# A two-layer decoder trunk on one core: unread 16-column products ahead of fifteen groups of products, and the norm's matrix moved by 64 bytes

## The chip, the cores and the metric

The kernel runs on one core of one Trainium2 chip. The time is that of one execution on the device, in microseconds (us); of several executions the median is taken. Most executions of this kernel agree within 0.3%.

## The reference, cut to what matters

One sequence of 512 tokens of width 1024 goes through two layers, all in float32.

```
h = rmsnorm(x, g) * (1 + scale) + shift            # scale, shift, gate: from c, one matrix-vector product per layer
layer 0: q, k, v, g = split(h @ w_in)              # 4 heads, q and k 256 wide, v and g 512 wide
         y = retention(rope(q), rope(k), v)        # chunked recurrence, here as scores over the whole sequence
         x = x + gate * ((silu(g) * groupnorm(y)) @ w_out)
layer 1: q, k = silu(causal_conv(h @ w_qk)); v, o  # stabilised mLSTM, 4 heads of the same widths
         x = x + gate * (groupnorm(sigmoid(o) * y) @ w_out)
both:    a, b = split(causal_conv(rmsnorm(x) ... @ w_up)); x = x + gate * ((silu(a) * b) @ w_down)
return rmsnorm(x, final_g)
```

## The kernel before, in words

Every float32 operand of a large product is split in two parts, high and low, of a rounded kind that TensorE takes in one pass (`hi`, `lo`; tiles `whi` and `wlo` for weights, `hh` and `hl` for the normed input, `t24h`, `t3h` and their low parts for sums of it). A product of 128x128 by 128x256 or by 128x512 is three instructions: high by high, high by low, low by high. In a profile row `out<-moving,stationary` the second name is the matrix that is loaded into the array before the product (LDWEIGHTS, rows of PEld), and the first is the operand that streams through it.

Most projections are done by a scheme with seven half-size products in place of eight (`seven`, `FoldUse`, `PairStream`, `ValueStream`; order of the products 1, 2, 6, 5, 7, 4, 3). A pair of 128-column tiles of query, key or gate weights is one such scheme with the weights stationary (output tiles `p1` and `p2`, shown as `p`). The values of a head are two such schemes side by side with the input stationary and the weights moving (output tiles `pv`). Each is 7 x 12 = 84 instructions of 256 columns. A head's queries and keys are two schemes after each other, 168 instructions; so are its gates, and so are its values. `heads` strings the heads together: queries, values, scores (`psc`), gates, attention (`pav`), output products (`po`). In the feed-forward part the same scheme runs for 18 tile pairs in `folded`. `boundary` does the last output products of a part in two halves of 256 columns and computes the next norm beside them: `SquareSum.root` multiplies the sums of squares by a constant matrix with 1/1024 in every cell (`ones["d"]`, tile `ones_d`, output `pms`), two instructions for each half.

In memory the input tiles (`slots`) and the constants start at multiples of 256 bytes. The weight tiles of the schemes, of `boundary` and of the products after it (`pf`) lie 64 bytes behind such a multiple: the tiles have 64 spare columns (`WPAD`) and are used from column 16 on (`OFF`). `ones_d` starts at a multiple of 256 bytes.

Two places already hold a product of 16 columns whose result nobody reads (`short_product`): the first scheme of each `folded` writes one into the quarter of its second output bank that VectorE fills later, and each `boundary` writes one into the last 16 columns of its first output bank.

The order of all instructions is made before the program is built, by a planner in the file (`Plan`): it plays the program through with a cost for each instruction, gives every instruction that feeds TensorE a due time, and lets each engine take what is due. Eight PSUM banks are handed out in turn; an instruction that reads a bank is due before the first product into the bank eight turns later.

Of the kernel before, what the change touches and what calls it, by code (L numbers as in the profile page):

```python
# [11 lines left out]
F32R = mybir.dt.float32r  # L12
# [4 lines left out]
P = 128  # L17
# [18 lines left out]
WPAD = 64  # L36
OFF = 16
# [349 lines left out]
def trunk(ctx: ExitStack, tc: tile.TileContext, xT, cb, pos, vec, ident, decay, zmask, ada, w_s0, w_in0, w_v0,  # L387
          w_o0, w_in1, w_v1, w_f1, w_o1, w_up, w_dn, out):
    nc = tc.nc
    const = ctx.enter_context(tc.tile_pool(name="const", bufs=1))  # L390
# [14 lines left out]
    def tile_of(pool, shape, dt, tag, name):  # L405
        return Buf(pool, shape, dt, tag, name, KINDS.get(tag, 0), tag == "ps")

    def slot(s, dt=F32, w=T):
        return tile_of(slots, [P, w], dt, "s", uid(s))
# [10 lines left out]
    def fixed(pool, shape, dt, name):  # L420
        b = tile_of(pool, shape, dt, name, name)
        b.get()
        return b

    plan = Plan()
    V, A, G, PE, S = (plan.engine(*p) for p in (("DVE", nc.vector), ("ACT", nc.scalar), ("POOL", nc.gpsimd),
                                                ("PE", nc.tensor), ("SP", nc.sync)))
# [3 lines left out]
    V.memset(fixed(const, [P, 32], F32, "pad")[:], 0.0)  # L431
    ones = {}
    for name, v in (("d", 1.0 / D), ("v", 1.0 / DV), ("1", 1.0)):
        o = fixed(const, [P, P], F32R, f"ones_{name}")
        V.memset(o[:].bitcast(F32), v)
        ones[name] = o

# [221 lines left out]
    def short_product(o, w, b):  # L659


        PE.matmul(o, w, b, start=True, stop=True, skip_group_check=True)

    def mm2(o, w, b, r=slice(None), start=True, stop=True):
        PE.matmul(o, w, b.hi[:, r], start=start, stop=False)
# [110 lines left out]
    class PairStream:  # L776
# [5 lines left out]
        def open(self, folds):  # L782
            self.f = folds
            b1, b2 = self.banks = bank("p1"), bank("p2")
            self.c11, self.c12, self.c21, self.c22 = b1[:, HA], b1[:, HB], b2[:, HA], b2[:, HB]

        def product(self, n, o, start):
            hi, hc, lo, lc = self.f.p[n]
            for k in range(4):
                b = self.terms(n, k)  # L790
                st, sp = start and k == 0, n in (2, 3, 4) and k == 3
                ch, cl = hi[:, hc + k * P : hc + k * P + P], lo[:, lc + k * P : lc + k * P + P]
                PE.matmul(o, ch, b[0], start=st, stop=False, skip_group_check=True)
                PE.matmul(o, ch, b[1], start=False, stop=False, skip_group_check=True)
                PE.matmul(o, cl, b[0], start=False, stop=sp, skip_group_check=True)

    class ValueStream(PairStream):
# [7 lines left out]
        def open(self, f):  # L805
            self.f = f
            x_, y_ = self.banks = bank("pv"), bank("pv")
            self.c11, self.c21, self.c12, self.c22 = x_[:, HA], x_[:, HB], y_[:, HA], y_[:, HB]

        def product(self, n, o, start):  # L810
            ts = slice(self.t * P, self.t * P + P)
            hi, lo = self.f.p[n]
            for k in range(4):
                b = self.terms(n, k)
                st, sp = start and k == 0, n in (2, 3, 4) and k == 3
                cs = slice(k * 256, k * 256 + 256)
                PE.matmul(o, b[0][:, ts], hi[:, cs], start=st, stop=False, skip_group_check=True)
                PE.matmul(o, b[0][:, ts], lo[:, cs], start=False, stop=False, skip_group_check=True)
                PE.matmul(o, b[1][:, ts], hi[:, cs], start=False, stop=sp, skip_group_check=True)

    def seven(use, streams, done, between=lambda j: None):


        fs = []

        def mk(n):
            def fn(w):
                if n == ORDER[0]:
                    for s in streams:
                        s.open(w[0])  # L830
                        fs.append(slot("fs"))
                for s, f in zip(streams, fs):
                    o = {1: s.c21, 2: s.c11, 5: s.c12, 3: s.c12}.get(n, s.c21)
                    s.product(n, o, n in s.starts)
                    if n in (1, 6, 7):
                        A.copy(f[:, HB if n == 6 else HA], s.c21)
                    if n == 7:
                        V.tensor_tensor(s.c22, s.c12, f[:, HA], op=ALU.add)
                    elif n == 2:
                        V.tensor_tensor(s.c11, s.c11, f[:, HA], op=ALU.add)  # L840
                    elif n == 3:
                        V.tensor_tensor(s.c12, s.c12, f[:, HB], op=ALU.add)
                if n == 3:
                    done(*[s.banks for s in streams])
            return fn
        for j, n in enumerate(ORDER):
            item([use], mk(n), j in FREE_STEPS)
            between(j)

    def fold_pairs(srcs, terms, thens, between=lambda j: None):  # L850

        def each(then):
            def done(bs):
                for b in bs:
                    then(b)
            return done
        for n, (src, then) in enumerate(zip(srcs, thens)):
            seven(FoldUse(src, n), [PairStream(terms, then)], each(then), lambda j: between(7 * n + j))

    def fold_values(src, terms, v, split, between=lambda j: None):  # L860

        def done(a, b):
            for ps in (a[0], b[0], a[1], b[1]):
                split(v, ps)
        seven(ValueFoldUse(src, 0), [ValueStream(terms, t) for t in range(2)], done, between)

    def folded(folds, h, terms, pairs, downs, quota):

# [668 lines left out]
    def ret_gate(i):  # L1537
        def then(ps):
            g = slot("g")
            A.activation(g[:], ps[:], AF.Silu)  # L1540
            R[i]["g"].append(g)
        return then
# [162 lines left out]
    sums0 = Sums(h0, {}, 0, 0)  # L1705

    def sums_early():
        sums0.make()
        sums0.turn()

    def pair_srcs(w, at):
        return [(w[at], w[at + 1]), (w[at + 2], w[at + 3])]

    def ret_q(i, between=nothing):
        thens = [half_pair(R[i], name, rope) for name in ("q", "k")]
        if i:
            fold_pairs(pair_srcs(w_in0, i * 8), sums0.terms, thens, between)
            return
        for n, then in enumerate(thens):
            for j in range(2):  # L1720
                proj_item(w_in0[i * 8 + 2 * n + j], h0, then, 2 * n + j in QLOW)
        item([], lambda w: sums_early())

    def ret_g(i):
        fold_pairs(pair_srcs(w_in0, i * 8 + 4), sums0.terms, [ret_gate(i)] * 2)

    def ret_v(i, between=nothing):
        fold_values(w_v0[i - 1], sums0.terms, R[i]["v"], center_split, between)
# [90 lines left out]
    def ml_gate(i):  # L1819
        def then(ps):  # L1820
            o = slot("o")
            A.activation(o[:], ps[:], AF.Sigmoid)
            M[i]["o"].append(o)
        return then
# [30 lines left out]

    def ml_q(i, between=nothing):
        thens = [lambda ps, name=name, n=iter((0, 1)): conv_then(i, name, next(n))(ps) for name in ("q", "k")]
        fold_pairs(pair_srcs(w_in1, 1 + i * 8), start1.sums.terms, thens, between)

    def ml_g(i):  # L1860
        fold_pairs(pair_srcs(w_in1, 5 + i * 8), start1.sums.terms, [ml_gate(i)] * 2)

    def ml_o(i):
        return pieces(lambda j: w_o1[i, j], 4, gate_col(1, 0), lambda k: M[i]["y"][k], i in O_ADDED)
# [4 lines left out]
    start1 = Start([w_in1[j] for j in (0, 5, 6, 7)], h1, 1, 0, [gates, ml_gate(0), ml_gate(0), ml_gate(0)], True)  # L1869
# [153 lines left out]
```

## Time and profile before

| | |
|---|---|
| median of 3 runs | 1483.56 us (1483.13 to 1486.03) |
| the profiled execution | 1483.41 us, of which the span of the trace is 1481.6 us |
| TensorE busy | 1461.3 us in 10468 matmuls |
| VectorE, ScalarE, GpSimd busy | 1268.1, 1075.9, 279.0 us |
| granted TensorE clock | 0.997 of full speed |

A busy time of an instruction holds the filling and draining of the array, which overlaps the next instruction; a row of 0.28 us for a product of 256 columns is therefore no price. The price is the distance from one start to the next, or the length of a merged row divided by its count.

### The profile page before, as it was taken

To read this page: it belongs to the slowest core of one execution; us is meant where nothing else is said; L and a number is where in the kernel's file an instruction comes from. 1 tells how busy PE (TensorE), PEld (TensorE's weight loads), DVE (VectorE), ACT (ScalarE), POOL (GpSimd) and SP (SyncE) were. 2 spreads that over 40 slices of the span, in tenths; PEclk is the share of its full clock that TensorE was granted. 3 is DMA by queue.
4 is the path that set the end of the run, shared out by engine and by line. 5 is a ranking of instruction groups with operands and counts; after the bars stand their busy time and mean duration, and the time that the engine had idled before them with its cause. 6 is when DMAs were issued, how large, how long until landed. Compare 5 with 4: busy or idle time off the path is not lost.

```text
span 1481.6 us, 27248 instructions
## 1 busy us (share of the span) xinstructions
PE 1461.3 (99%) x10468; PEld 1368.8 (92%) x10468; DVE 1268.1 (86%) x2136; ACT 1075.9 (73%) x1606; POOL 279.0 (19%) x313
## 2 busy tenths in 40 slices
PE   9999999999999999999999999999999999999997
PEld 6799999998999999999999998999889899999997
DVE  7999979777989889898897999999889887777786
ACT  5678768777577676676668986989856876767662
POOL 0334132322111111111001222132211111111100
PEclk9999999999999999999999999999999999999998
DMA  9868989888798899999457895888687887888751
GB/s 363 252 175 207 282 209 230 224 250 212 206 215 215 241 261 258 265 261 266 118 180 171 207 246 144 208 221 199 205 239 201 213 219 194 194 208 191 190 125 58
DMA packets 93268, 315.65 MB, mean 213 GB/s; under 512 B 12225, under 2 KB 14657, under 8 KB 93138
## 3 DMA queue, kind: packets, MB, share of 16 engines
q0 software_dynamic: 32112, 116.54, 42.2%
q1 hardware_dynamic: 60738, 197.11, 38.3%
q8 instruction: 82, 1.34, 0.4%
q10 hardware_dynamic: 288, 0.27, 0.1%
q14 instruction: 48, 0.39, 0.1%
HBM read 195.23 MB, written 2.12 MB: 133 GB/s over the span
## 4 chain that ended last, share of the span: by engine, by line
PE 86%; DMA 7%; DVE 3%; ACT 2%; issue 2%; POOL 0%; DVEq 0%; ACTq 0%; SPq 0%; POOLq 0%
PE p L383 36%; PE po L383 27%; PE pv L383 9%; PE pav L383 4%; PE pp L383 3%; PE pf L383 3%; DMA wlo<-raw 2%; PE psc L383 2%; DMA raw<-w_in 1%; DMA wb<-w_up 1%; DMA raw<-w_dn 1%; PE pst L383 1%; DMA wlo<-wa 1%; DMA raw<-w_up 1%; PE pms L383 1%
## 5 line engine op out<-in xcount | busy, mean ns | idle before, releaser
L383 PE MATMUL p<-hh,whi 128*128 128x256 f32 (+1 forms) x994 | 275.6, 278 | 1.9 <-DVE p L383 1.9
L383 PE MATMUL p<-hl,whi 128*128 128x256 f32 x992 | 275.1, 277 | 0.0
L383 PE MATMUL p<-hh,wlo 128*128 128x256 f32 x992 | 273.4, 277 | 0.0
L383 ACT ACTIVATE wlo<-whi 128x1024 fp32r<-128x1024 f32 x223 | 235.0, 1057 | 39.8 <-PE po L383 15.1
L383 PEld LDWEIGHTS p<-hh,whi 128*128 128x128 f32 x994 | 187.1, 188 | 2.8 <-DVE p L383 2.3
L383 PEld LDWEIGHTS p<-hl,whi 128*128 128x128 f32 x992 | 186.7, 188 | 0.4
L383 PEld LDWEIGHTS p<-hh,wlo 128*128 128x128 f32 x992 | 185.6, 188 | 0.0
L383 PE MATMUL p<-t24h,whi 128*128 128x256 f32 x744 | 165.0, 279 | 4.1 <-ACT fs L383 3.1
L383 PE MATMUL po<-ggl,whi 128*128 128x512 f32 (+1 forms) x448 | 153.3, 343 | 0.0
L383 PE MATMUL po<-ggh,wlo 128*128 128x512 f32 (+1 forms) x448 | 153.1, 343 | 0.0
L383 PE MATMUL po<-ggh,whi 128*128 128x512 f32 (+1 forms) x448 | 152.4, 343 | 0.0
L383 ACT CAST whi<-raw 128x1024 fp32r<-128x1024 f32 (+1 forms) x117 | 118.0, 1019 | 44.8 <-DMA raw<-w_s 10.5
L383 PE MATMUL p<-t24l,whi 128*128 128x256 f32 x496 | 137.5, 277 | 0.0
L383 DVE SCALAR_TENSOR_TENSOR x<-po,mod,x 128x512 f32<-128x512 f32 (+1 forms) x184 | 113.0, 628 | 23.2 <-PE po L383 22.7
L383 PEld LDWEIGHTS p<-t24h,whi 128*128 128x128 f32 x744 | 126.3, 188 | 6.9 <-ACT fs L383 3.9
L383 DVE SCALAR_TENSOR_TENSOR ada<-ada,c_ext 128x1025 f32<-128x1025 f32 x96 | 119.5, 1246 | 6.5 <-DMA ada<-ada 6.4
L383 POOL DMA_DIRECT2D wlo<-wa x62 | 53.8, 867 | 355.4 <-ACT wlo L383 223.4
L383 PE MATMUL po<-yh,whi 128*128 128x256 f32 (+1 forms) x354 | 116.0, 329 | 0.3 <-ACT o L383 0.3
L383 PE MATMUL po<-yl,whi 128*128 128x256 f32 (+1 forms) x352 | 115.7, 329 | 0.0
L383 PE MATMUL po<-yh,wlo 128*128 128x256 f32 (+1 forms) x352 | 115.6, 329 | 0.0
L383 DVE SCALAR_TENSOR_TENSOR cv<-p,vecs,cv 128x511 f32<-128x511 f32 (+1 forms) x144 | 106.4, 744 | 9.9 <-ACT cv L383 9.2
L383 ACT CAST whi<-ws 128x1024 fp32r<-128x1024 f32 x86 | 90.0, 1050 | 28.5 <-DVE ws L383 23.5
(287 smaller groups left out, 4422.0 us busy)
## 6 DMA issues: line engine op xcount, KB each, us to landing
ada<-ada SPq DMA_DIRECT2D x96, 512.5 KB, 7.4
wlo<-ws POOLq DMA_DIRECT2D x68, 512.0 KB, 6.9
wlo<-wa POOLq DMA_DIRECT2D x62, 512.0 KB, 6.3
wlo<-wt POOLq DMA_DIRECT2D x44, 512.0 KB, 6.9
wlo<-raw POOLq DMA_DIRECT2D x41, 512.0 KB, 8.4
wa<-w_up SPq DMA_DIRECT2D x36, 512.0 KB, 6.9
wb<-w_up SPq DMA_DIRECT2D x36, 512.0 KB, 6.2
raw<-w_o SPq DMA_DIRECT2D x32, 512.0 KB, 6.6
```

What stands on the lines that cost most here:

```text
L383: getattr(c.obj, c.name)(*[real(v) for v in c.a], **{key: real(v) for key, v in c.k.items()})
```

## The change

Three edits. First, `ones_d` gets 64 spare columns and is used from column 16 on, so that it lies 64 bytes behind a multiple of 256, as the weight tiles do; what follows it in memory moves by 256 bytes. Second, `PairStream` and `ValueStream` get a method `lead`, which issues one product of 16 columns with the operands of the group's first product, into the quarter `c22` of the second output bank, which VectorE overwrites later. For pairs this bank is the one that the first product writes anyway; for values it is the second bank of the first stream, which the group's products reach with their fourth step. Third, `seven` calls it for the first scheme of a group where the caller asks: the values of heads 1 to 3 and the gates of heads 1 to 3 in both layers, the queries of head 2 in layer 0, and of heads 0 and 2 in layer 1. That is fifteen leads. The planner counts them with no occupancy (`occ = 0.0`).

```diff
-        o = fixed(const, [P, P], F32R, f"ones_{name}")
+        off = OFF if name == "d" else 0
+        o = fixed(const, [P, P + WPAD * (off > 0)], F32R, f"ones_{name}")[:, off : off + P]
...
     def short_product(o, w, b):
-        PE.matmul(o, w, b, start=True, stop=True, skip_group_check=True)
+        return PE.matmul(o, w, b, start=True, stop=True, skip_group_check=True)
...
     class PairStream:
...
+        def lead(self, n):
+            hi, hc, _, _ = self.f.p[n]
+            short_product(self.c22[:, :16], hi[:, hc : hc + P], self.terms(n, 0)[0][:, :16]).occ = 0.0
...
     class ValueStream(PairStream):
...
+        def lead(self, n):
+            ts = slice(self.t * P, self.t * P + P)
+            short_product(self.c22[:, :16], self.terms(n, 0)[0][:, ts], self.f.p[n][0][:, :16]).occ = 0.0
...
-    def seven(use, streams, done, between=lambda j: None):
+    def seven(use, streams, done, between=lambda j: None, lead=False):
...
                         fs.append(slot("fs"))
+                    if lead:
+                        streams[0].lead(n)
...
-            seven(FoldUse(src, n), [PairStream(terms, then)], each(then), lambda j: between(7 * n + j))
+            seven(FoldUse(src, n), [PairStream(terms, then)], each(then), lambda j: between(7 * n + j),
+                  lead and not n)
...
-        seven(ValueFoldUse(src, 0), [ValueStream(terms, t) for t in range(2)], done, between)
+        seven(ValueFoldUse(src, 0), [ValueStream(terms, t) for t in range(2)], done, between, True)
...
-            fold_pairs(pair_srcs(w_in0, i * 8), sums0.terms, thens, between)
+            fold_pairs(pair_srcs(w_in0, i * 8), sums0.terms, thens, between, i == 2)
...
-        fold_pairs(pair_srcs(w_in0, i * 8 + 4), sums0.terms, [ret_gate(i)] * 2)
+        fold_pairs(pair_srcs(w_in0, i * 8 + 4), sums0.terms, [ret_gate(i)] * 2, lead=True)
...
-        fold_pairs(pair_srcs(w_in1, 1 + i * 8), start1.sums.terms, thens, between)
+        fold_pairs(pair_srcs(w_in1, 1 + i * 8), start1.sums.terms, thens, between, i in (0, 2))
...
-        fold_pairs(pair_srcs(w_in1, 5 + i * 8), start1.sums.terms, [ml_gate(i)] * 2)
+        fold_pairs(pair_srcs(w_in1, 5 + i * 8), start1.sums.terms, [ml_gate(i)] * 2, lead=True)
```

The order of instructions changes in two ways. TensorE gets its fifteen rows. And because a value group's lead needs its bank three steps earlier than a product did, what reads that bank is due earlier, and the planner shifts other work on VectorE and ScalarE around it.

TensorE at the values of head 1 in layer 0, before (the end of the attention product `pav`, then the group; `pv_1260` is the first output bank):

```order
L383 MATMUL pav_1239<-sh_1043,vh_758 128x256
L383 MATMUL pav_1239<-sl_1056,vh_758 128x256
L383 MATMUL pav_1239<-sh_1043,vl_1012 128x256
L383 MATMUL pv_1260<-whi_1015,hh_239 128x256
L383 MATMUL pv_1260<-wlo_1034,hh_239 128x256
```

and now (`pv_1260` is now the second bank, `pv_1262` the first):

```order
L383 MATMUL pav_1239<-sh_1043,vh_758 128x256
L383 MATMUL pav_1239<-sl_1056,vh_758 128x256
L383 MATMUL pav_1239<-sh_1043,vl_1012 128x256
L383 MATMUL pv_1260<-whi_1015,hh_239 128x16
L383 MATMUL pv_1262<-whi_1015,hh_239 128x256
L383 MATMUL pv_1262<-wlo_1034,hh_239 128x256
```

One product of 16 columns stands ahead of the group; the rest of the row is as it was.

VectorE just ahead of the same place, before (`rp` is the rotation that reads the key and query banks `p_224` and `p_223`, `ws` and `wlo` prepare the value weights):

```order
L383 TENSOR_TENSOR ws_1202<-wv_883,wv_886 128x1024
L383 TENSOR_TENSOR wlo_1221<-wv_1026,whi_1124 128x1024
L383 TENSOR_TENSOR ws_1235<-wv_1026,ws_1169 128x1024
L383 TENSOR_TENSOR rp_1250<-p_224_962,sin_776 128x512
L383 TENSOR_TENSOR rp_1257<-p_224_962,cos_790 128x512
L383 TENSOR_TENSOR p_223_980<-p_223_980,fs_994 128x256
```

and now:

```order
L383 TENSOR_TENSOR ws_1202<-wv_883,wv_886 128x1024
L383 TENSOR_TENSOR rp_1221<-p_224_962,sin_776 128x512
L383 TENSOR_TENSOR rp_1227<-p_224_962,cos_790 128x512
L383 TENSOR_TENSOR wlo_1237<-wv_1026,whi_1124 128x1024
L383 TENSOR_TENSOR ws_1250<-wv_1026,ws_1169 128x1024
L383 TENSOR_TENSOR p_223_980<-p_223_980,fs_994 128x256
```

The two reads of the bank `p_224` have moved ahead of two preparations of weights. Over the whole program some 80 rows of VectorE and as many of ScalarE have changed places like this, all within the heads; five transfers have changed places on SP's queue and eleven rows on GpSimd's.

TensorE at the values of head 1 in layer 1, before (`pden` is two products of 512 columns for the denominator):

```order
L383 MATMUL pden_10114<-sumsh_10078,ones_81 128x512
L383 MATMUL pden_10114<-sumsl_10090,ones_81 128x512
L383 MATMUL pv_10120<-whi_9863,hh_8793 128x256
L383 MATMUL pv_10120<-wlo_9874,hh_8793 128x256
L383 MATMUL pv_10120<-whi_9863,hl_8805 128x256
```

and now:

```order
L383 MATMUL pden_10122<-sumsh_10094,ones_81 128x512
L383 MATMUL pv_10125<-whi_9871,hh_8800 128x16
L383 MATMUL pv_10125<-whi_9980,hh_8800 128x256
L383 MATMUL pden_10122<-sumsl_10114,ones_81 128x512
L383 MATMUL pv_10125<-wlo_9996,hh_8800 128x256
```

Here the lead and one product of the group have moved between the two products of `pden`.

More of the change, by code (lines that the diff above doesn't have):

```diff
@@ L848, in seven, with fold_pairs @@
             between(j)
-    def fold_pairs(srcs, terms, thens, between=lambda j: None):
+    def fold_pairs(srcs, terms, thens, between=lambda j: None, lead=False):
         def each(then):
```

## The prediction

> **What bounds the kernel now.** I read the page first, then what TensorE waited for, then the chain of waits in order of time. From the page and the waits:
>
> ```profile
> PE 1461.3 (99%) x10468; PEld 1368.8 (92%) x10468; DVE 1268.1 (86%) x2136; ACT 1075.9 (73%) x1606; POOL 279.0 (19%) x313
> ...
> PE 86%; DMA 7%; DVE 3%; ACT 2%; issue 2%; POOL 0%; DVEq 0%; ACTq 0%; SPq 0%; POOLq 0%
> ...
> PE p L383 <- ACT fs L383: 3.1, 4, 1.3
> PE p L383 <- DVE p L383: 2.9, 4, 1.3
> ```
>
> TensorE is busy 99% of the span, and its waits inside the layers come to some 6 us in 8 places, none over 1.3 us. So what a stream of products costs is its pace, start to start. The chain of waits (start, length, what, count) gives the pace as length by count:
>
> ```profile
> 119.13 19.79 PE pv L383 x168
> ...
> 143.26 16.33 PE p L383 x144
> ...
> 191.82 16.96 PE p L383 x144
> 208.78 2.12 PE pv L383 x18
> 210.90 2.73 PE p L383 x24
> 213.64 3.40 PE pv L383 x30
> ...
> 217.50 14.13 PE pv L383 x120
> ...
> 235.51 16.96 PE p L383 x144
> ...
> 302.81 11.20 PE p L383 x95
> ...
> 470.29 8.17 PE p L383 x72
> ...
> 711.38 18.70 PE po L383 x165
> ...
> 730.32 12.72 PE po L383 x108
> ...
> 747.75 18.14 PE pf L383 x154
> ...
> 919.39 15.55 PE p L383 x132
> ...
> 962.69 16.96 PE p L383 x144
> ...
> 1030.25 7.08 PE p L383 x60
> ...
> 1118.03 13.43 PE po L383 x114
> ...
> 1458.02 12.74 PE po L383 x108
> ```
>
> All are products of 256 columns at full clock, yet there are two paces. 16.33 us for 144 is 113.4 ns, as are 8.17 for 72 and 18.70 for 165. 16.96 for 144 is 117.8 ns, as are 19.79 for 168, 14.13 for 120 and 12.72 for 108. The two rows of 144 are the same code in different heads (gates of head 1, queries of head 2). A stream keeps its pace to its end, so the pace is set where the stream begins. The difference is **4.4 ns a product**, and this is what the change works on.
>
> **How a stream gets its pace.** The timeline of TensorE shows two places. The first is the product of 16 columns that opens the first `folded`:
>
> ```profile
> 446.55 0.39 PE L383 MATMUL pp<-hh,wlo 128*128 128x512 f32 x1
> 446.78 0.39 PE L383 MATMUL p<-hh,whi 128*128 128x16 f32 x2
> 447.01 0.28 PE L383 MATMUL p<-hl,whi 128*128 128x256 f32 x1
> 447.13 0.28 PE L383 MATMUL p<-hh,wlo 128*128 128x256 f32 x1
> 447.25 0.28 PE L383 MATMUL p<-hh,whi 128*128 128x256 f32 x1
> ```
>
> The second row is the 16 columns and the first real product. Behind them the stream runs at 113.5 ns (8.17 for 72). A stream of 512 columns stands ahead of them, as it does ahead of the queries at 191.82, which have no such product and run at 117.8. From 446.78 to 447.25 lie three real products, which take 0.34 at the fast pace, so **a lead costs 0.13 us**. It is a new price on the chain: nothing covers it.
>
> The second place is the norm's matrix in a boundary:
>
> ```profile
> 388.25 0.28 PE L383 MATMUL po<-yl,whi 128*128 128x256 f32 x1
> 388.36 0.28 PE L383 MATMUL pms<-ssh,ones_d 128*128 128x256 f32 x1
> 388.48 0.28 PE L383 MATMUL po<-yh,wlo 128*128 128x256 f32 x1
> ...
> 389.07 0.28 PE L383 MATMUL po<-yh,whi 128*128 128x256 f32 x1
> ...
> 402.14 0.28 PE L383 MATMUL pf<-hh,whi 128*128 128x256 f32 x1
> ...
> 406.39 0.28 PE L383 MATMUL pf<-hh,whi 128*128 128x256 f32 x1
> ...
> 425.00 0.39 PE L383 MATMUL pp<-hh,whi 128*128 128x512 f32 x1
> ```
>
> Up to `pms` the starts are 0.11 apart, from it on 0.12. The 111 products from 389.07 take 13.07 us, 117.7 ns each, and the 158 from 406.39 take 18.61, 117.8 ns. The second boundary shows the same (fast `po` at 711.38, slow at 730.32 and 747.75). In `po` and `pf` the matrix lies 64 bytes off the operand's grid and in `pms` it does not; nothing else is different there.
>
> **The change part by part.** *The matrix, 64 bytes later.* Then `pms` has the same relation of addresses as its neighbours, and I expect the stream to keep 113.4. Slow products behind `pms`, as the order has them: 307 in the first boundary with its `pf`, 300 in the second, 310 in the third, 108 at the end. 1025 x 4.4 ns = 4.5 us. Not all reaches the end. The first 1.35 us runs up to 425, and TensorE then waits at 449 to 452 for the low parts of the first `folded`, whose chain left TensorE at 393.86:
>
> ```profile
> 393.86 7.89 DMA raw<-w_up
> ...
> 441.34 8.55 DMA wlo<-wa
> ```
>
> It has passed only 40 of the 307 products by then, so most of this gain goes into that wait: between 0.2 and 1.35 is kept, I take 0.4, by the row of the chain. The third (1.36) meets a wait of the same kind ahead of the second `folded`; there I take 0.8. The second (1.3) and the last (0.5) meet none. Kept: 0.4 + 1.3 + 0.8 + 0.5 = **3.0 us**, bounds 2.0 and 4.5.
>
> The Trainium skill speaks against this edit: in "SBUF — State Buffer", section "Who interferes with whom", TensorE has two independent read ports, one for the moving operand and one for the weights, and only the pair that VectorE and GpSimd share contends. By it no offset can change the pace, and the edit is worth 0. The trace does not agree: one stream goes from 113.4 to 117.8 ns at a product that differs in its matrix's offset alone.
>
> *The fifteen leads.* They cost 15 x 0.13 = 1.95 us. They can earn only where the group is slow now. By the chain: values of head 1 in layer 0 168; queries of head 2 144; values of head 2 18 and 120; gates of head 2 144; gates of head 3 95; layer 1: queries of head 2 132, gates of head 2 144, gates of head 3 60. The queries of head 0 in layer 1 are slow up to a wait of TensorE at 801 and fast behind it:
>
> ```profile
> 793.20:801.00 7.80, 7.80 (x69) 1.00 1.01 202
> ```
>
> 69 products that last 0.28 us touch these 7.80 us, 117 ns each. That gives 69 more. The gates of head 1 run fast already (143.26), and a lead there only costs.
>
> The values are broken up by other products, and the chain shows what that does. From the weights-stationary `p` to `pv` the pace is kept (191.82 slow, 208.78 slow; 210.90 fast, 213.64 fast), from `pv` to `p` it turns over (208.78 slow, 210.90 fast), and two products of `pvar` at 217 turn it again (213.64 fast, 217.50 slow). So with a lead the values of head 2 in layer 0 would be fast for 18, slow for 24 and 30, fast for 120: 84 gained of the 138. The values of head 3 in both layers, and of heads 1 and 2 in layer 1, which the order breaks up in the same way, gain about 0 by this rule.
>
> Sum: 168 + 144 + 84 + 144 + 95 + 69 + 132 + 144 + 60 = 1040 x 4.4 ns = **4.6 us**. That a lead makes a `pv` stream fast is not shown before; without it 168 and 84 fall away, 1.1 us. Net of the leads' price 2.6 us, bounds 1.5 and 2.9 (the parts of the gates of head 3 that the rows above don't hold).
>
> *The planner's new order.* It holds within the heads. I bound it by the present waits, at most 1.3 us each: a loss of two such, or a gain of 0.5 where one of the present ones goes away. I take a loss of 0.6.
>
> Sum against the profiled execution: 1483.41 - 3.0 - 4.6 + 1.95 + 0.6 = **1478.4 us**. The execution is 0.15 below the median, so I forecast 1478.4 for the median too.
>
> **The rivals.** *The lead of a value group waits.* It writes the second bank of the first stream, which products reach only with the fourth step, 72 products or 8.2 us later. At the values of head 1 in layer 0 the last reader of that bank was VectorE's rotation:
>
> ```profile
> 118.22 0.68 DVE L383 TENSOR_TENSOR rp<-p,cos 128x512 f32<-128x512 f32 x1
> ```
>
> It ends at 118.90, 0.2 us ahead of the group. Behind a waiting lead stands all of TensorE. If six leads wait 1.5 us each, 9 us are lost: 1478.4 + 9 = 1487.4, slower; from 0.85 us each the gain is gone. Against it: in the new order these reads stand ahead of two preparations of weights, so they end about 2 us earlier. Chance 0.09.
>
> *The paces are not set by offset or lead.* Then 1.95 us of leads are paid for nothing: 1485.4, with the new order 1486.0. For it stands that the gates of head 1 became fast without a lead. Against it stand the `pms` rows. Chance 0.08. The rule of the Trainium skill in "SBUF — State Buffer", section "Who interferes with whom", would give this time too.
>
> *The gain comes and is given back.* All paces are as I say, but the waits grow: VectorE or ScalarE are late in the new order, and the low parts ahead of the `folded` absorb more. With 2.0 kept of the matrix, 1.5 of the leads and 2.6 lost to two new waits: 1482.5. Chance 0.15.
>
> **How the numbers follow.** My forecast, a gain of 3 to 8 us, has 0.68. The least time is all of both gains, without loss: 1483.4 - 4.5 - 2.9 - 0.5 = 1475.5; I take 1474.5 as the lower end, since the rule for broken values may be too strict. The upper end takes in the third rival: 1484.0. About 0.2% (3 us) is what can be told from no change. Faster than that, below 1480.6: the forecast and a little of the third rival, 0.70. Within it: the rest of the third, the second and a part of the first, 0.20. Slower, above 1486.5: 0.10.
>
> **What would show it.** The `po` and `pf` streams behind `pms` at 113.4 ns in the chain of waits, and the two starts at `pms` 0.11 apart, show the matrix right. The rows of 144 at 191.82, 235.51 and 962.69 with 16.33 us, and the 168 of `pv` with about 19.05, show the leads right; 16.96 shows them wrong. Waits of `pv` on VectorE or ScalarE in TensorE's list would show the first rival; a longer wait of `p` on `fs` or on VectorE, the third. The prediction is wrong if the paces come as said and the time does not follow, for then the absorption was sized wrong.

## The result, and the profile after

The change makes the kernel slower: 1486.58 us median against 1483.43, over 22 executions of each, a ratio of **1.0022** (95% interval 1.0015 to 1.0029), or +3.2 us. Forecast were 1478.4, and 1484.0 at most.

The profiled execution of the change took 1487.83 us with a span of 1485.8. Its page, busy times and then the share of the chain by engine:

```profile
PE 1461.1 (98%) x10483; PEld 1367.8 (92%) x10483; DVE 1266.2 (85%) x2136; ACT 1076.2 (72%) x1606; POOL 283.1 (19%) x313
...
PE 81%; DMA 9%; DVE 4%; issue 3%; ACT 2%; SPq 0%; POOL 0%; DVEq 0%; POOLq 0%; ACTq 0%
```

TensorE holds 81% of the chain where it held 86%, and DMA 9% instead of 7%. That is no measure of the loss: where TensorE waits for a transfer, the chain follows the whole transfer. What TensorE waited for in the layers is small (total, times, longest):

```profile
PE p L383 <- DVE p L383: 3.8, 6, 1.4
PE p L383 <- ACT fs L383: 2.5, 3, 1.2
...
PE p L383 <- DMA wlo<-wa: 0.6, 1, 0.6
PE pf L383 <- DMA wlo<-raw: 0.4, 1, 0.4
```

VectorE kept TensorE waiting six times instead of four, and two waits for low parts are new. All four rows come to 7.3 us, where the two of before came to 6.0. The paces stand in the chain of waits (start, length, what, count), whose rows of a group with a lead count one product more:

```profile
119.82 19.90 PE pv L383 x169
...
144.08 14.25 PE p L383 x121
...
210.29 2.23 PE pv L383 x19
...
215.25 3.40 PE pv L383 x30
...
219.12 14.13 PE pv L383 x120
...
237.13 17.07 PE p L383 x145
...
304.90 10.90 PE p L383 x96
...
408.46 18.61 PE pf L383 x158
...
749.11 17.46 PE pf L383 x154
...
803.39 23.35 PE p L383 x196
...
923.19 16.78 PE p L383 x145
...
966.88 14.26 PE p L383 x121
...
1036.88 7.19 PE p L383 x61
...
1124.62 12.92 PE po L383 x114
...
1462.72 12.25 PE po L383 x108
```

Two things are to be seen. Behind the norm's matrix the streams are fast now: 17.46 for 154 is 113.4 ns (18.14 before), 12.92 for 114 and 12.25 for 108 the same (13.43 and 12.74 before). One of them isn't: the 158 at 408.46 still take 18.61, behind the wait for `wlo<-raw` (0.42 us, at 404.66), which the kernel before did not have there. In the heads most leads did nothing or harm: the values at 119.82, the gates of head 2 at 237.13 and at 966.88 stay at 117.8 ns, the gates of head 3 at 1036.88 too, and the gates of head 1, fast before (143.26, 16.33 for 144), are slow (144.08). Of the named groups the gates of head 3 in layer 0 (304.90, 113.5 ns) gained, and, counted start by start, the queries of head 2 there. Counted from the starts in the trace, 1946 products of `p` and `pv` in the heads ran at the slow pace before, 2268 do after: 1.4 us lost where 4.6 were to be won.

### The profile page after: what moved, and what is told of

Its sections match the earlier page's. It is cut to its first block, busy times and chain, and to the rows that moved or that the text cites. A ratio compares the mean times of both kernels' runs of the same rounds, so it can differ in the third digit from the quotient of the medians.

```text
span 1485.8 us, 27279 instructions
## 1 busy us (share of the span) xinstructions
PE 1461.1 (98%) x10483; PEld 1367.8 (92%) x10483; DVE 1266.2 (85%) x2136; ACT 1076.2 (72%) x1606; POOL 283.1 (19%) x313
## 4 chain that ended last, share of the span: by engine, by line
PE 81%; DMA 9%; DVE 4%; issue 3%; ACT 2%; SPq 0%; POOL 0%; DVEq 0%; POOLq 0%; ACTq 0%
PE p L383 33%; PE po L383 22%; PE pv L383 8%; PE pp L383 5%; PE pf L383 4%; PE pav L383 4%; DMA ada<-ada 2%; PE psc L383 2%; PE pst L383 2%; DMA wlo<-raw 1%; DMA raw<-w_dn 1%; DMA wlo<-wa 1%; DMA raw<-w_in 1%; DVE ada L383 1%; ACT whi L383 1%
```

## The experiments

Seventeen kernels were run, those of a group on one chip beside the kernel before. Ratios are to that. A single profiled execution can lie 2 to 4 us from its kernel's median (`leads` 1490.81 against 1487.20), so times are compared by ratio and profiles only for paces and for which waits there are.

| run | what | median us | ratio (95%) |
|---|---|---|---|
| matrix | the norm's matrix alone | 1479.65 | 0.9982 (0.9973 to 0.9991) |
| leads | leads and their order alone | 1487.20 | 1.0032 (1.0020 to 1.0045) |
| order_no_leads | the change without the 15 products, in its order | 1483.33 | 1.0010 (1.0001 to 1.0019) |
| leads_old_order | the change in the order of before | 1483.61 | 1.0005 (0.9996 to 1.0013) |
| order_layer0 | order_no_leads, layer 0 only | 1480.14 | 0.9980 (0.9970 to 0.9989) |
| order_layer1 | order_no_leads, layer 1 only | 1483.96 | 1.0009 (1.0000 to 1.0018) |
| order_v1 | the same, head 1 of layer 1 only | 1483.50 | 1.0005 (0.9996 to 1.0013) |
| order_v2 | head 2 only | 1479.14 | 0.9980 (0.9971 to 0.9989) |
| order_v3 | head 3 only | 1478.00 | 0.9972 (0.9962 to 0.9983) |
| double_leads | leads_old_order, each lead twice | 1481.08 | one execution |
| triple_leads | each lead three times | 1483.36 | one execution |
| two_matrices | matrix, and pvar's matrix too | 1481.28 | 0.9989 (0.9979 to 0.9999) |
| late_slots | two_matrices, keys and values too | 1486.48 | 1.0026 (1.0016 to 1.0036) |
| query_leads | matrix and three query leads | 1478.31 | 0.9968 (0.9956 to 0.9980) |
| wide_leads | query_leads and six openers of 512 columns | 1478.80 | 0.9981 (0.9968 to 0.9994) |
| chosen | query_leads and four chosen openers | 1478.09 | 0.9972 (0.9962 to 0.9982) |
| both_gains | query_leads in the order of order_v3 | 1476.92 | 0.9953 (0.9940 to 0.9967) |

My theory after the result: the matrix earned what was forecast, and the loss has two parts, the planner's new order and the leads themselves. The first four runs take the change apart.

### The matrix alone, and the leads alone

```diff
+        off = OFF if name == "d" else 0
+        o = fixed(const, [P, P + WPAD * (off > 0)], F32R, f"ones_{name}")[:, off : off + P]
```

> Only the norm's matrix 64 bytes later, no 16-column products, the order of before. Theory (the matrix earns what it was forecast to, and the loss comes from the rest of the change): some 1000 products of po and pf behind pms go from 117.8 to 113.4 ns, of which waits take about 1, so 3.5 us less than before, 1480.0 (1479 to 1481). Rival (the matrix's gain is lost in later waits whatever stands in the heads): within 1 us of before, 1483. The heads keep their paces in both.

> The fifteen 16-column products and the order that comes with them, the matrix where it was. Theory (the two edits add up): the change's +3.1 us and the matrix's 3.5 come to +6.6, so 1490.0 (1489 to 1491). Rival (the loss is made by both together, for instance since the matrix's 256 bytes move every later tile): about 1485, the leads' own price alone.

The matrix alone: 0.9982, so 2.7 us less (1.3 to 4.0), as forecast. Its chain:

```profile
390.07 12.58 PE po L383 x111
...
406.95 17.91 PE pf L383 x158
...
746.95 17.45 PE pf L383 x154
...
1457.09 12.25 PE po L383 x108
```

All four at 113.4 ns, among them the 158 that the change lost again; in this run no wait stands ahead of them. In other runs with the matrix moved single streams of `pf` turn slow behind a wait or a longer gap between two starts (in `order_v1` all three, 18.61, 18.14 and 18.61 us), so the gain isn't kept whole in every execution. The leads alone, with the order that comes with them: 1.0032, +4.7 us. The expected 1490.0 was too high; the matrix's gain beside the leads is 1.0032 - 1.0022, 1.5 us, which the intervals do not tell from 2.7. The rival, that leads alone cost only their price (1485), is too low.

### The order and the products, apart

`order_no_leads` plans the leads and leaves them out when the program is written. `leads_old_order` plans without them and writes each one ahead of its group's first product; those of the values write the first bank's quarter `c11`.

```diff
 # order_no_leads
-        for n in self.order():
+        for n in (n for n in self.order() if self.calls[n].eng != 'PE' or self.calls[n].occ):
 # leads_old_order
+            for c in (*self.ahead.get(n, ()), self.calls[n]):
...
-            short_product(self.c22[:, :16], self.terms(n, 0)[0][:, ts], self.f.p[n][0][:, :16]).occ = 0.0
+            short_product(self.c11[:, :16], self.terms(n, 0)[0][:, ts], self.f.p[n][0][:, :16], True)
```

> Planned as the change, with its matrix, and in its order on every engine, but the fifteen products are left out when the program is written (they are unread, so the outputs are all computed). Theory (the planner's order costs some 3.8 us in new waits of TensorE in the heads, the leads' price and the paces behind them the other 2 to 3): 1483.5 (1482.5 to 1485), with the same waits at 797 to 802, 877 to 880, 981 to 985 and 1051. Rival (the waits come from the leads' lateness, the order itself costs nothing): 1480, as with the matrix alone.

> The order of before on every engine, the matrix of the change, and the fifteen products put right ahead of their groups when the program is written (those of the values write a part of the group's first bank). Theory A (the order makes the waits; a lead makes a group fast only behind a stream of 512 columns, and slow elsewhere): queries of head 2 (layer 0) and of heads 0 and 2 (layer 1) at 113.4 ns, gates of head 1 in both layers at 117.8; 1.8 us of leads and about 0.5 us net of paces against the matrix's 3.5: 1482.3 (1481 to 1483.5). Theory B (a lead turns over the pace that its group would have had, fast to slow and slow to fast): gates of head 1 in both layers slow, but values of head 1, gates of head 2 in both layers, and the queries named all fast: 1479.8. Rival (the order has no part in the loss): 1486.

The order without the products is 1.0010, against 0.9982 for the matrix alone: **the order costs 4.2 us** (2 to 6, from the two intervals). The products on top of it cost 1.0022 - 1.0010, 1.8 us; in the order of before they cost 1.0005 - 0.9982, 3.4, so that the order on top of them costs 2.5. The intervals do not tell 1.8 from 3.4, or 2.5 from 4.2. So both parts are there. That -2.7 + 4.2 + 1.8 gives the change's +3.2 proves nothing more, since each step starts where the one before it ends. Theory A's 1482.3 and theory B's 1479.8 for `leads_old_order` were both too low, B's by more.

What moves the order is one detail. The planner makes an instruction that reads a bank due before the first product into the bank eight turns later (lines 256 and 257). A pair's lead writes the bank that the group's first product writes anyway. A value's lead in `c22` makes itself the first product of the second bank, 72 products ahead of the one that was. Planned with the value leads in `c11`, or with the pairs' leads alone, every engine's order is that of before, row for row; the whole new order comes from the six value leads' choice of quarter.

### Where the order loses

```diff
-        fold_values(w_f1[i - 1], start1.sums.terms, M[i]["v"], plain_split, between)
+        fold_values(w_f1[i - 1], start1.sums.terms, M[i]["v"], plain_split, between, i == 1)   # order_v1; 2, 3; or all of a layer
```

> The norm's matrix, and the plan with the values' 16-column products of layer 0 alone, which are then left out of the program (the outputs are all computed): the change's order in the heads of layer 0, before's order in layer 1. Theory (the new waits stand in the heads of layer 1): 0.5 us over the matrix alone, 1480.2. Rival (each of the six value groups costs the same): 1481.5.

> The same with the values of layer 1 alone: the change's order in the heads of layer 1, before's in layer 0. Theory (the new waits of some 3 us stand here): 1483.0, with TensorE waiting near 797 to 802 and 877 to 880 as in the run with the whole new order. Rival (each of the six groups costs the same): 1481.5.

By the times, layer 0's order costs nothing (0.9980 against 0.9982), layer 1's all of it (1.0009, as with both). TensorE's waits in the run with layer 0's order:

```profile
PE p L383 <- DVE p L383: 2.0, 3, 1.0
PE p L383 <- ACT fs L383: 1.6, 2, 1.0
```

and in the run with layer 1's:

```profile
PE p L383 <- DVE p L383: 4.6, 8, 1.3
PE p L383 <- ACT fs L383: 2.4, 4, 1.0
PE p L383 <- DMA wlo<-wa: 1.2, 1, 1.2
```

3.6 us against 8.2. These totals alone don't place the loss: the execution with the matrix alone has 7.2 (3.6 for VectorE, 3.2 for `fs`, 0.4 for a low part) at the same ratio as layer 0's. The length of a stretch does. Counted from the starts in the traces, heads 1 to 3 of layer 1, from the first value product of head 1 to the boundary, take 242.2 us before, 242.8 with the matrix alone, 241.7 with layer 0's order, and 246.1 with layer 1's and 246.2 with both. So the order loses some 3 to 4 us there. The largest new wait in the timeline of TensorE in the run with layer 1's order:

```profile
876.64 0.39 PE L383 MATMUL p<-t3h,whi 128*128 128x256 f32 x1 [0.44 <-ACT fs L383]
879.52 0.38 PE L383 MATMUL p<-hh,wlo 128*128 128x256 f32 x1 [1.24 <-DMA wlo<-wa]
```

> The norm's matrix, and the plan with the 16-column product of head 1's values in layer 1 alone, which is then left out of the program (the outputs are all computed). Theory (the loss of the order in layer 1 is the wait near 879 for low parts whose high parts ScalarE makes later, and it comes with head 1's values): 2 to 4 us over the norm's matrix alone, 1482.5. Rival (each new order loses a little, wherever it begins): about 1481, as the next two.

> The same with head 2's values in layer 1 alone. Theory (head 1's is the one that loses): as the norm's matrix alone, 1479.8. Rival (each new order loses a little): about 1481.

> The same with head 3's values in layer 1 alone. Theory (head 1's is the one that loses): 1480, a little more for the waits near 997 to 1029. Rival (each new order loses a little): about 1481.

Of the three value groups only head 1's loses: 1.0005, 3.4 us over the matrix alone. Head 2's costs nothing; head 3's is 1.5 us better, which the intervals do not tell from nothing. The rival, that any new order loses a little, falls. The stretch named above takes 244.1 us with head 1's group and 241.2 with head 2's or head 3's, so head 1's alone makes about half of what the whole layer loses there, and the rest is seen only in the runs with all three. A part of head 1's is seen on ScalarE. The high part of the gates' weights in the run with the matrix alone:

```profile
856.65 1.06 ACT L383 CAST whi<-wa 128x1024 fp32r<-128x1024 f32 x1 [0.59 <-DMA wa<-w_in]
```

and, with the steps that follow it on ScalarE, in the run with head 1's group in the plan:

```profile
862.89 1.07 ACT L383 CAST whi<-wa 128x1024 fp32r<-128x1024 f32 x1
...
865.36 1.07 ACT L383 ACTIVATE wlo<-whi 128x1024 fp32r<-128x1024 f32 x1
```

whose chain goes on with the DMA that adds the weights to that negative, at whose end TensorE's timeline has a wait:

```profile
866.74 10.36 DMA wlo<-wa
```

```profile
877.13 0.38 PE L383 MATMUL p<-hh,wlo 128*128 128x256 f32 x1 [0.98 <-DMA wlo<-wa]
```

In the order of before ScalarE makes this part as soon as `wa` has landed. In the new order it comes 6.2 us later, behind steps that followed it before (the high part of `wt`, copies out of banks, squares); its negative goes to that DMA, which takes 10.4 us, and TensorE, which needs the sum at 876.15, waits 0.98 us (1.24 in the run with all of layer 1). The late start is not the only way to this wait: with the order of before `double_leads` has it too, 0.98 us, after a transfer of 12.5. A second wait of this run, 1.13 us for `wlo<-wt` at 1049.61, stands in none of the others named here. The waits for VectorE and ScalarE are not longer in this run than with the matrix alone (4.7 us against 6.8). What else makes up the 3.4 stays open; in this execution slow streams are part of it, since all three `pf` are slow, where `order_v2` has two and `order_v3` one.

### What a lead does to the pace

`leads_old_order` has every instruction where it was before, so it shows the leads alone, and the next two runs issue each lead twice and three times.

```diff
-        plan.ahead.setdefault(len(plan.calls), []).append(c)
+        plan.ahead[len(plan.calls)] = [c, c]          # triple_leads: [c, c, c]
```

> As the fifteen products in the order of before, but each of them issued twice. Theory A (a 16-column product gives the stream a pace by what stands ahead of it: fast behind 512 columns of weights, else slow): the same paces as with one, gates of head 1 slow in both layers, queries of head 2 fast; 1.8 us more than with one, 1485.4. Theory B (each such product turns the pace over): gates of head 1 fast, queries of head 2 in layer 0 at 117.8 again.

> As with the fifteen products issued twice, but each issued three times. Theory B (each such product turns the pace over, counted from the place's own): queries of head 2 in layer 0 fast, gates of head 1 slow in both layers, gates of head 2 at 117.8; about 1486. Theory C (what counts is whether one stands there or several): the paces of the run with two, gates of head 1 fast, queries slow; about 1483.

Rows of the chain with one lead (gates of head 1 and of head 2 in layer 0, queries of head 2 in layer 1):

```profile
144.10 17.07 PE p L383 x145
...
237.18 17.07 PE p L383 x145
...
920.55 15.37 PE p L383 x133
```

the same three with two leads:

```profile
144.78 16.55 PE p L383 x146
...
237.73 16.89 PE p L383 x146
...
919.95 15.77 PE p L383 x134
```

and with three, the queries of head 2 in layer 0 (193.07) among them:

```profile
143.53 17.30 PE p L383 x147
...
193.07 16.68 PE p L383 x147
...
236.82 17.01 PE p L383 x147
...
920.86 15.60 PE p L383 x135
```

A lead costs 0.11 us (17.07 less 16.96). Without it the groups take, for none, one, two and three leads:

| group | 0 | 1 | 2 | 3 | paces |
|---|---|---|---|---|---|
| gates of head 1, layer 0 (144) | 16.33 | 16.96 | 16.33 | 16.97 | fast, slow, fast, slow |
| queries of head 2, layer 1 (132) | 15.55 | 15.26 | 15.55 | 15.27 | slow, half fast, slow, half fast |
| gates of head 2, layer 0 (144) | 16.96 | 16.96 | 16.67 | 16.68 | slow, slow, half fast, half fast |

In the first two **each product of 16 columns turns the pace over**, theory B, and theory A, that it gives a pace of its own, falls. The gates of head 1 in layer 1, the queries of head 0 there and the queries of head 2 in layer 0 do the same where they begin; waits follow in them. Theory B does not hold everywhere: the gates of head 2 go in steps of two, in both layers, the values of head 1 start slow with any number, and the gates of head 3 start slow with one and two (with three, slow in layer 0 and fast in layer 1), though in the change one lead started those of layer 0 fast. Each column is one execution, but paces come back: the queries of head 2 in layer 1 start fast and turn after 67 products in seven of the eight runs that have one or three leads there, and stay fast in the eighth. "Half fast" is 67 products, start by start; behind the sixth step of the first scheme the stream turns slow. I do not know why the places differ or why it turns there.

### Is it the relation of addresses?

The matrix's edit suggests that what stands ahead, scores and attention with both operands on one grid, sets the slow pace. `two_matrices` moves the matrix of `pvar` as well; `late_slots` puts 16 of the 62 slots 64 bytes later and keys and values there, in the order of before.

```diff
-        off = OFF if name == "d" else 0
+        off = OFF if name in "dv" else 0
 # late_slots
+            if tag == "s" and self.at >= NSLOTS - NLATE:
+                pool = LATE[1]
```

> No 16-column products of the change, the order of before; besides the norm's matrix also the one of the heads' variance (pvar) lies 64 bytes later. Theory (what turns a pace is a product whose two operands have another relation of addresses than its neighbours): the 30 values ahead of pvar at 213 and the 120 behind it at 217 get the same pace, the gates of head 1 are no longer turned by pvar from slow to fast; the sum of the paces moves by less than 1 us either way: 1479.7 (1478.7 to 1480.7). Rival (pvar turns the pace by its 512 columns or its two starts): the paces of the run with the norm's matrix alone, value streams turned at pvar as there.

> As the run before it, and 16 of the 62 slots lie 64 bytes later; keys and values, the matrices of the scores and of the attention, are put there where one is free, everything else on the others, in the order of before on every engine. Theory (a product of 256 columns whose matrix and operand both lie on the grid takes 117.8 to 120 ns and hands the slow pace to what follows): psc and pav go from 120 to about 113.4 ns per 256 columns, which is 2 us over the heads, and the gates and values behind them start fast, up to 5 us of the 8.7 us that the heads lose to the slow pace: 1474.5 (1473 to 1477). Rival (the grid matters in the norms alone, or the slow pace comes from the way a stream starts): psc and pav stay at 120, time as the run before, 1479.7.

The values around `pvar` in the run with the norm's matrix alone, where `pvar` turns them from slow (118 ns) to fast (113.3):

```profile
214.97 3.54 PE pv L383 x30
218.51 0.47 PE pvar L383 x2
218.97 13.60 PE pv L383 x120
```

and with both matrices moved, where it does not (118, then 117.8):

```profile
215.15 3.53 PE pv L383 x30
218.69 0.47 PE pvar L383 x2
219.16 14.13 PE pv L383 x120
```

So the relation of addresses does turn a stream, here as in `pms`. (The rival, that `pvar` turns it by its 512 columns or its two starts, falls at this place: both are the same in the two runs.) But the gates of head 1 still came out fast behind the moved `pvar`, and the time is no better (0.9989). With keys and values moved, a stream of `folded` in layer 0, the scores of head 2 in layer 1, and a stream of `folded` in layer 1 with what stands ahead of it:

```profile
588.78 8.18 PE p L396 x72
...
958.16 3.81 PE psc L396 x24
...
1254.92 2.76 PE po L396 x12
1257.68 8.48 PE p L396 x72
```

The scores took 3.88 where their keys stayed on the grid; they did not become fast, and the theory that their grid makes their pace falls. Worse, the time is 1.0026. From 1250 on every stream of `folded` in layer 1 runs at 117.8 ns (8.48 for 72, where 8.17 is the rule), some 4 us. The addresses in the built program go with it: of the gated tiles that output products of 512 columns read ahead of each stream (the row `po` x12, four tiles), the low part of the last (`ggl`) lies in a late slot in all three groups from 1250 to 1426. The last product but one ahead of the stream then has its operand 64 bytes off its matrix's grid, where otherwise both lie on one grid. In layer 0 two late ones stand second and third of the four (582 to 634), and the streams there stay fast (588.78). That fits the theory for these streams, with a place: what counts is the relation of addresses in the last products ahead. It also corrects the form in which I had put it: both operands on one grid is what stands there ahead of the fast streams, so it is a change of the relation that goes with the turn, and not the one grid itself. No run was made for this alone.

### Versions with the gains alone

`query_leads` keeps the matrix and the three leads of query groups in the order of before. `wide_leads` adds openers of 512 columns on one grid, `chosen` adds two and three leads at the gates of head 2 and one wide opener at head 3's. `both_gains` puts `query_leads` into the order of `order_v3`.

```diff
 # query_leads (in ml_g alike, and not in fold_values)
-        fold_pairs(pair_srcs(w_in0, i * 8 + 4), sums0.terms, [ret_gate(i)] * 2, lead=True)
+        fold_pairs(pair_srcs(w_in0, i * 8 + 4), sums0.terms, [ret_gate(i)] * 2)
 # wide_leads, ahead of six groups
+                short_product(self.banks[1][:], hi[:, :P], hi[:, : 2 * 256], True)
 # chosen (-1: the wide opener); in ml_g (0, 0, 3, -1)
+        fold_pairs(pair_srcs(w_in0, i * 8 + 4), sums0.terms, [ret_gate(i)] * 2, lead=(0, 0, 2, -1)[i])
```

> The norm's matrix, the order of before and only the three 16-column products of query groups (head 2 of layer 0, heads 0 and 2 of layer 1), which all stand behind a stream of 512 columns. Theory (there a lead makes the stream fast): 144 products of head 2 in layer 0, some 67 of each of the others at 113.4 ns, so up to 1.2 us against a price of 0.36: 0.3 to 0.8 less than with the matrix alone, 1479.1. Rival (a wait in the stream draws its pace anew, so the gain doesn't last): 1480.0.

> As the three query products in the order of before, and an unread product of 512 columns, its matrix and its operand on one grid as pvar's, ahead of six groups that are still slow: values of head 1, gates of heads 2 and 3, in both layers. Theory (pvar made the gates of head 1 fast behind slow scores since it has 512 columns on one grid): all six start at 113.4 ns; 838 products x 4.4 ns = 3.7 us against a price of 6 x 0.23 = 1.4, so 2.3 less than with the three alone, 1476.0. Rival (it is the pair of them, or the place, that turned the pace): the groups stay slow, 1479.7.

> The norm's matrix, the order of before, the three query products, and ahead of four groups of gates the opener that the runs so far showed to start them fast: two products of 16 columns at head 2 of layer 0, three at head 2 of layer 1, one of 512 columns at head 3 of both. Theory (the place and the number of products set the pace): gates of head 2 fast for 67 products or more, of head 3 for some 100, so 2 us of paces for 1.1 of price: 0.5 to 0.9 less than with the three query products, 1477.6. Rival (waits draw the paces anew, the price stays): 1479.2.

> The order of the run planned with head 3's values of layer 1 (that product left out of the program, the outputs all computed), the norm's matrix and the three query products. Theory (the gain of that order, 1.5 us over the norm's matrix alone, and that of the three products, 1.3 to 2, stand in different heads and add up): 1476.3. Rival (the two gains are draws of the same waits and don't add up): 1478.2, as each alone.

`query_leads` is 0.9968, a little better than expected; the queries of head 2 in layer 0 run at 113.4 ns throughout, while the second `pf` is slow behind its wait for `wlo<-raw`:

```profile
192.48 16.45 PE p L383 x145
...
743.89 18.14 PE pf L383 x154
```

The wide opener turned the gates of head 3 in both layers and left the other four groups slow (the gates of head 2 with their opener 17.19 for 145), and the time, 0.9981, isn't better; the intervals do not tell it from 0.9968. In `chosen` the paces came as the table says (gates of head 2 16.90 for 146), yet the time is that of `query_leads`: the half us that was expected is below what can be told. `both_gains` has 0.9953, 7.0 us less than before, faster than both kernels and the least ratio of all. Adding the two gains would give 0.9958, but the intervals of its two parts reach down to 0.9962 and 0.9956, so that they add up fits and isn't shown.

## Why the prediction was wrong

| term | forecast | measured |
|---|---|---|
| the matrix | -3.0 | -2.7 |
| price of the leads | +1.95 | +1.7 (15 x 0.11) |
| paces that the leads set | -4.6 | +0.1 in the new order, +1.7 in that of before (remainders) |
| the planner's order | +0.6 | +4.2 (2 to 6) |

The third row is what the runs with leads leave beside their price, 1.8 - 1.7 and 3.4 - 1.7, each uncertain by nearly 2. Counted start by start in one execution each, the change has some 320 slow products of the heads more than the kernel before, which is the 1.4 us above. `leads_old_order` has some 60 fewer in the heads, so its +1.7 is no loss of paces there: in its profiled execution the second boundary's `po` and `pf` were slow behind a wait. What the leads did to the paces is thus known to 2 us only; that the 4.6 did not come is clear.

*The matrix, 64 bytes later* was right in mechanism and size: with no wait ahead, `po` and `pf` keep 113.4 ns past `pms`. "It meets a wait" was right too, with a turn that I had not seen: a wait not only absorbs a gain, it can give a stream the slow pace again (408.46). The rule of the Trainium skill in "SBUF — State Buffer", section "Who interferes with whom", by which the two read ports of TensorE are independent, would have left this edit at 0; the trace does not agree, 17.46 us against 18.14 for the same 154 products with the matrix moved.

*A lead costs 0.13 us* was right (0.11).

*The failed step is that a lead makes its group fast.* I took it from one place, the first `folded`, where a lead stands behind products of 512 columns, and applied it to fifteen groups. By the counts of one, two and three, a lead at five of the places turns over the pace that the place would have given. Behind products of 512 columns that is slow to fast, the only kind I had seen; at the gates of head 1 it is fast to slow. "A lead there only costs" named these gates and missed that it could cost 0.6 us of pace each. At the gates of head 2, right behind scores, one lead does nothing. At head 2 of layer 0 two leads cancel: its queries came in fast and the lead of its values turned that back, so the values and the `p` between them keep the paces of before (210.29, 215.25, 219.12), where the sum had 84 gained. Of the nine groups summed to 1040 products, two gained nearly in full, the queries of head 2 and the gates of head 3 in layer 0, and the queries of head 2 in layer 1 gained half. The queries of head 0 in layer 1 gained their 69 ahead of the wait. The same trace of before held a warning: the gates of head 1 were fast without a lead, so what stands ahead sets a pace, and a lead could not be the only thing that counts.

*"A stream keeps its pace to its end"* failed too. The queries of head 2 in layer 1 turn slow after 67 products, and the queries of head 0 there leave a wait slow in the change (803.39, 23.35 for 196) that they left fast before; with the matrix alone they leave it slow too, so that need not be the lead's doing.

*The planner's new order* was mis-sized, 4.2 us for 0.6. The bounds, a loss of two present waits or 2.6, reach only the lower end of it: I had bounded new waits by the sizes of present ones and not by how late a needed tile would come. ScalarE's high part moved by 6.2 us, ahead of a DMA of 10.4 us; that row of the new order priced against that DMA would have pointed at one of the new waits, some 1 us. Where the rest of the 4.2 comes from is shown only as far as the heads of layer 1.

*The rivals.* Value leads that wait for their bank: no lead waited. But the bank was the right place: the claim on it was paid in the plan, 72 products early, instead of at the lead. Paces not set by offset: refuted by `po` and `pf`. "The gain comes and is given back" was nearest, with its two new waits at 2.6, but it kept 1.5 us of leads, which never came.

## What to carry to other kernels

An instruction that costs nothing in a planner still claims its buffer: put it where it claims what the next real instruction claims, and the order stays. A remedy seen at one place is worth trying at one place: what these short products do differs from place to place, so each has to be tried on its own, and groups that are already fast are the ones to keep away from. A new order is to be priced by the tile that comes later in it, with the transfer behind that tile, not by the waits that are there already.

## What the hardware showed that was not expected

- Products of 256 columns have two paces, 113.4 and 117.8 ns, and at five places in the heads an unread product of 16 columns turns the one that its place would have given into the other: one, two and three of them gave slow, fast, slow at a place that is fast without, and the opposite at one that is slow. At the gates of head 2 it takes two (16.96, 16.96, 16.67 us for 144 with none, one, two), and the values of head 1 stay slow with any number.
- A product whose two operands have another relation of addresses, modulo 256 bytes, turns the stream that it stands in (`pms`: 18.14 us for 154 against 17.45; `pvar`: 14.13 for 120 against 13.60). One that stands just ahead went with a turned stream in one run (`ggl`: 8.48 us for 72 against 8.17). Moving the keys changed the scores' own 24 products by 0.07 us at most.
- A wait of TensorE can draw the pace anew: behind the same wait of 0.51 us for `wlo<-raw`, near 744, the 154 products of the second `pf` came out fast with the matrix alone (17.45) and slow in `query_leads` (18.14).
